# The first gate and value units of a feed-forward up projection, run unit after unit or feature tile by feature tile over four PSUM accumulators

## The chip, the cores and the metric

The kernel runs on one NeuronCore of a Trainium2 chip, in one launch. The metric is device time in microseconds (us). The engines are TensorE (PE in the rows; PEld is its weight load), VectorE (DVE), ScalarE (ACT), GpSimd (POOL) and SyncE (SP, which here only issues DMAs). A stage is read on the profiled execution, and times are compared as medians of several executions.

## The reference

Two layers of a decoder block on 256 tokens of width 1024, in float32. The change touches only the first half of each layer's feed-forward part:

```python
for l in range(DEPTH):                                   # DEPTH = 2
    ...                                                  # attention of two kinds
    x = x + mixed @ w_out[l]
    h = rmsnorm(x, norm_ffn_g[l])
    g_in, u = jnp.split(h @ w_up[l], 2, axis=-1)         # 1024 -> 2 x 2816
    x = x + (jax.nn.silu(causal_dwconv(g_in, conv_w[l], conv_b[l])) * u) @ w_down[l]
```

`causal_dwconv` is a convolution of three taps over the tokens. The row factor of the norm, `rsqrt(mean(x*x) + eps)`, is one number per token.

## The kernel before, in words

Activations are kept features by tokens: `x` is `[128, 8, 256]`, eight feature tiles of 128 features with 256 tokens each. Float32 products are made of three passes: weights and activations are each split into a high part `hi` (rounded to the short float that TensorE takes at full rate) and a rest `lo`, and `hi*hi + hi*lo + lo*hi` is summed in PSUM. So every weight that arrives by DMA in a `raw` buffer (five buffers, half a unit each) is first cast by ScalarE (`hi`, L242) and then subtracted by VectorE (`lo`, L243). A weight unit holds 256 output features; `next_unit(3)` asks for two units beyond the current one and issues their casts and subtractions at once.

The feed-forward part of a layer:

- `out_proj` adds the attention's output to `x`, feature tile by feature tile (L1065, two instructions for a tile). After each tile, `feed` makes the tile's `u`: `hi` on ScalarE (L314), `lo` on VectorE (L315), and its squares (L337), which GpSimd and, for the last tile, VectorE (L345, tile `fin`) sum for the norm.
- `ffn_up` goes through 11 column tiles `c`. Each has a gate unit (columns of `g_in`) and a value unit (columns of `u`), and each unit two halves of 128 columns. A half is 8 feature tiles k times 3 passes, 24 matmuls of 128x256 in one PSUM accumulator. `u` is not yet multiplied by the norm's row factor; that comes on the way out of PSUM.
- `rstd_col` forms the factor per token: two matmuls sum `fin` over the features (L356), VectorE (L358), GpSimd (a power, L359) and ScalarE (two diagonal blocks `dg`, L363). `rstd_row` spreads it over all partitions with one matmul (L369) and a ScalarE copy (`rb`, L371).
- `post_g` takes the gate unit out of PSUM (`g = acc * rb`, L1093), convolves it (L1096, L1097, L1099), forms the silu (L1101, L1102) and multiplies by `rb` again on GpSimd (L1103). The value unit is multiplied in (L1117) and the result is split into `act` (L300).

For c = 0 the kernel has an order of its own: the gate unit's two halves take turns feature tile by feature tile, one in an `acc` buffer, one in an `att` buffer, since the last tiles of `u` are still being made. Then comes the value unit, and in it, as hooks in front of matmul 3, 27 and 33, `rstd_col`, `rstd_row` and `post_g(0)`. For c > 0 a unit's two halves share one `acc` buffer, one half after the other.

PSUM has eight banks: the pool `acc` has three buffers, the pool `att` five. `out_proj` uses one `acc` buffer for each feature tile. The program is laid down in the order of the code, but a scheduler of the framework then orders each engine's instructions by its own estimates; each engine runs them strictly in that order. With c = 1 and on, the loop has settled into a pattern that repeats for each c.

Of the kernel before, what the change touches and what calls it, by code (L numbers as in the profile page):

```python
# [15 lines left out]
ALU = mybir.AluOpType  # L16
# [3 lines left out]
P = 128  # L20
D = 1024
S = 256
# [142 lines left out]
def block_kernel(ctx, tc, x_in, xo_in, ws, g_norm, g_rope, pos, w2, conv, rope_c, ropec_c, mask_c, misc_c, out):  # L165
    nc = tc.nc
    V, A, G, T = nc.vector, nc.scalar, nc.gpsimd, nc.tensor
# [5 lines left out]
    def acc():  # L173
        t = acc_p.tile([P, 512], F32, name="acc")
        return t

    def att():
        t = att_p.tile([P, 512], F32, name="att")
        return t
# [38 lines left out]
    def prepare(upto):  # L218
        while nxt[0] < len(units) and nxt[0] <= upto:
            i = nxt[0]  # L220
            u = units[i][1:]
            ffn = u[0] in ("up", "down")
            if ffn and ffn_pool[0] is None:
                return
            if u[0] == "w1":
                split[i] = [load_half(i, c0, UW // 2) for c0 in (0, UW // 2)]
                nxt[0] += 1
                continue
            w = _unit_width(u)
            pool, nb = (ffn_pool[0], 1) if ffn and ffn_turn(i) else (com, 2)  # L230
            hi = pool.tile([P, UW], F32R, name="hi", bufs=nb)
            lo = pool.tile([P, UW], F32R, name="lo", bufs=nb)
            step = w // 4 if (i, w // 4) in early else w // 2
            for c0 in range(0, w, step):
                if (i, c0) in early:
                    raw = early.pop((i, c0))
                else:
                    raw = load_half(i, c0, step)
                c = slice(c0, c0 + step)

                def halve(h=hi[:, c], l=lo[:, c], r=raw):
                    A.copy(h, r)  # L242
                    V.tensor_sub(l, r, h.bitcast(F32))  # L243
                pend.append((i, halve))
            split[i] = (hi, lo)
            nxt[0] += 1
# [3 lines left out]
    def flush(upto):  # L250
        while pend and pend[0][0] <= upto:
            pend.popleft()[1]()

    def next_unit(ahead=2):
        i = ui[0]
        ui[0] += 1
        flush(i)
        prepare(i + ahead - 1)
        flush(i)
        if ahead != 2 or units[i][1] in ("up", "down", "out") :  # L260
            flush(i + ahead - 1)
        return split.pop(i)
# [35 lines left out]
    def split_evac(hi, lo, src):  # L298
        A.copy(hi, src)
        V.tensor_sub(lo, src, hi.bitcast(F32))  # L300
# [3 lines left out]
    def new_u(pool=com, name="hT"):  # L304
        u = pool.tile([P, 2, 8, S], F32R, name=name)
        sums.clear()
        return u
# [59 lines left out]
    def rstd_row():  # L367
        ps = att()
        T.matmul(ps[:, 0:S], ones, sums["dg"], start=True, stop=True)  # L369
        rb = com.tile([P, S], F32, name="rb", bufs=1)  # L370
        A.copy(rb, ps[:, 0:S])  # L371
        return rb

    def run(mms, hooks={}):
        for i, f in enumerate(mms):
            if i in hooks:
                hooks[i]()
            f()

    def feat_major(o, hi, lo, src, ms, nk):  # L380
        todo = []
        for k in range(nk):
            todo += [(o, hi[:, k, ms], src[:, 0, k], k == 0, False), (o, hi[:, k, ms], src[:, 1, k], False, False),
                     (o, lo[:, k, ms], src[:, 0, k], False, k == nk - 1)]
        return [lambda a=a: T.matmul(a[0], a[1], a[2], start=a[3], stop=a[4]) for a in todo]  # L385
# [684 lines left out]
    def ffn_up(l, pool, u, act):  # L1070
        cw = pool.tile([P, NFT, 4], F32, name="cw")
        nc.sync.dma_start(cw, conv[l].rearrange("p (f i) -> p f i", i=4))
        box = {}

        def unit(hooks, first=False):
            hi, lo = [z.rearrange("p (k n) -> p k n", k=8) for z in next_unit(3)]
            p1 = acc()
            outs = [p1[:, 0:S], att()[:, 0:S] if first else p1[:, S:]]
            lists = [feat_major(outs[mt], hi, lo, u, slice(mt * P, (mt + 1) * P), 8) for mt in range(2)]
            if first:  # L1080
                mms = [f for i in range(0, 24, 3) for ls in lists for f in ls[i:i + 3]]
            else:
                mms = lists[0] + lists[1]
            run(mms, hooks)
            return outs if first else [p1]

        def post_g(c, p1):
            z = pool.tile([P, 2, S], F32, name="z", bufs=3)
            g = pool.tile([P, 2, S], F32, name="g", bufs=2)
            rb = box["rb"][:, None, :].to_broadcast([P, 2, S])  # L1090
            for i, z1 in enumerate(p1):
                n = 2 // len(p1)
                V.tensor_tensor(g[:, i * n:(i + 1) * n], z1.rearrange("p (a q) -> p a q", a=n), rb[:, :n], op=ALU.mult)  # L1093
            for mt in range(2):
                f = 2 * c + mt
                A.activation(z[:, mt], g[:, mt], AF.Identity, bias=cw[:, f, 3:4], scale=cw[:, f, 2:3])  # L1096
                V.scalar_tensor_tensor(z[:, mt, 1:], g[:, mt, :S - 1], cw[:, f, 1:2], z[:, mt, 1:],  # L1097
                                       op0=ALU.mult, op1=ALU.add)
                V.scalar_tensor_tensor(z[:, mt, 2:], g[:, mt, :S - 2], cw[:, f, 0:1], z[:, mt, 2:],  # L1099
                                       op0=ALU.mult, op1=ALU.add)  # L1100
            A.activation(g, z, AF.Tanh, scale=0.5)  # L1101
            V.scalar_tensor_tensor(z, g, 1.0, z, op0=ALU.add, op1=ALU.mult)  # L1102
            G.tensor_tensor(z, z, rb, op=ALU.mult)  # L1103
            box["z"] = z

        def second(c, pg):
            return {10: lambda: post_g(c, pg)}

        for c in range(11):
            if c == 0:  # L1110
                pg = unit({}, True)
                pu = unit({3: rstd_col, 27: lambda: box.update(rb=rstd_row()), 33: lambda: post_g(0, pg)})
            else:
                pg = unit({})
                pu = unit(second(c, pg))
            z = box["z"]
            V.tensor_tensor(z, z, pu[0].rearrange("p (a q) -> p a q", a=2), op=ALU.mult)  # L1117
            split_evac(act[:, 0, 2 * c:2 * c + 2], act[:, 1, 2 * c:2 * c + 2], z)

    def ffn_down(l, act):  # L1120
# [47 lines left out]
    for l in range(DEPTH):  # L1168
        with tc.tile_pool(name=f"attn{l}", bufs=1, reuse_waits="tile") as pool:
            mT = attention_layer(l, pool, hT)  # L1170
        with tc.tile_pool(name=f"ffn{l}", bufs=1, reuse_waits="tile") as pool:
            ffn_pool[0] = pool
            u = new_u(pool, "u")
            act = pool.tile([P, 2, NFT, S], F32R, name="act")
            pad = pool.tile([P, 16], F32, name="pad")
            G.memset(pad, 0.0)
            hT = out_proj(l, u, mT)
            ffn_up(l, pool, hT, act)
            hT = ffn_down(l, act)
            ffn_pool[0] = None  # L1180
# [32 lines left out]
```

## Time and profile before

| | us |
|---|---|
| median of 3 runs (954.5 to 956.36) | 955.96 |
| profiled execution, its own time | 956.27 |
| span in the profile, first to last instruction | 954.5 |
| PE busy (share of the span) | 934.4 (98%) |
| DVE busy | 762.1 (80%) |
| ACT busy | 570.0 (60%) |
| POOL busy | 151.8 (16%) |
| busy share of the DMA queue that brings the weights | 52.3% of 16 engines |

An engine's busy time is the time in which one of its instructions runs. Matmuls are pipelined and their ends are modelled, so the gaps between matmuls are better read from their starts than from the busy share. Starts in the rows are in us from the span's start; the first layer's feed-forward part begins at 297.49 and the second layer's at 768.95.

### The profile page before, as it was taken

The numbers are of one execution on the slowest core, as the hardware profiler recorded it, in microseconds if no ns is written. First come the engines' busy times: TensorE is split into PE (matmuls) and PEld (weight loads), VectorE is DVE, ScalarE is ACT, GpSimd is POOL, SyncE is SP. The second block draws the span as 40 slices with busy tenths as digits, with TensorE's granted clock in tenths as the row PEclk, the third lists the DMA queues.
The fourth block names the chain that finished last, engine by engine and source line by source line (L and its number), as shares of the span: only waits on it lengthen the run. The fifth ranks groups of instructions, "written<-read, shape, count | busy, mean of one in ns | idle before, by whom it ended". The sixth has DMA issues, their size and how long they took to land.

```text
span 954.5 us, 18604 instructions
## 1 busy us (share of the span) xinstructions
PE 934.4 (98%) x7102; PEld 851.2 (89%) x7102; DVE 762.1 (80%) x1722; ACT 570.0 (60%) x1164; POOL 151.8 (16%) x177
## 2 busy tenths in 40 slices
PE   8999999999999999999999999999999999999998
PEld 6778887879999999999988787878799999999998
DVE  5999967987778899986569998688976988988742
ACT  5768756665556555555456876576645655555431
POOL 2230112221002111110143311131300121111000
DMA  8643456435457565666455335644354565666660
GB/s 288 238 142 123 160 178 229 140 111 167 154 154 228 182 201 179 200 197 198 145 170 197 113 118 198 209 144 161 117 181 155 161 221 176 198 196 199 198 209 19
DMA packets 48330, 165.95 MB, mean 174 GB/s; under 512 B 6128, under 2 KB 7664, under 8 KB 48112
## 3 DMA queue, kind: packets, MB, share of 16 engines
q1 hardware_dynamic: 46656, 163.17, 52.3%
q10 hardware_dynamic: 1584, 1.59, 0.5%
q8 instruction: 56, 0.92, 0.4%
q14 instruction: 34, 0.28, 0.1%
HBM read 163.69 MB, written 1.05 MB: 173 GB/s over the span
## 4 chain that ended last, share of the span: by engine, by line
PE 75%; DVE 13%; ACT 6%; DMA 2%; issue 2%; POOL 2%; ACTq 0%; DVEq 0%; POOLq 0%
PE acc L385 26%; PE acc L296 5%; PE acc L294 5%; PE acc L295 5%; DVE lo L243 5%; PE acc L1131 4%; PE acc L1133 4%; PE acc L1132 4%; PE att L620 3%; PE att L625 3%; PE acc L1006 2%; PE acc L1008 2%; PE acc L1007 2%; ACT hi L242 2%; PE acc L1042 2%
## 5 line engine op out<-in xcount | busy, mean ns | idle before, releaser
L243 DVE TENSOR_TENSOR lo<-raw,hi 128x1024 fp32r<-128x1024 f32 (+2 forms) x294 | 369.0, 1271 | 54.5 <-ACT hi L242 52.5
L242 ACT CAST hi<-raw 128x1024 fp32r<-128x1024 f32 (+2 forms) x294 | 293.9, 1030 | 163.0 <-PE acc L295 52.8
L385 PE MATMUL acc<-u,hi 128*128 128x256 f32 x1376 | 238.4, 278 | 1.2 <-DVE u L315 1.2
L385 PEld LDWEIGHTS acc<-u,hi 128*128 128x128 f32 x1376 | 208.1, 188 | 1.8 <-DVE u L315 1.6
L385 PE MATMUL acc<-u,lo 128*128 128x256 f32 x688 | 190.5, 277 | 0.0
L294 PE MATMUL acc<-hi,hT 128*128 128x512 f32 (+1 forms) x384 | 152.6, 397 | 2.7 <-ACT hi L242 2.7
L296 PE MATMUL acc<-lo,hT 128*128 128x512 f32 (+1 forms) x384 | 149.0, 389 | 4.9 <-DVE lo L243 4.9
L295 PE MATMUL acc<-hi,hT 128*128 128x512 f32 (+1 forms) x384 | 147.4, 385 | 0.0
L385 PEld LDWEIGHTS acc<-u,lo 128*128 128x128 f32 x688 | 129.1, 188 | 0.0
L1133 PE MATMUL acc<-act,lo 128*128 128x256 f32 x352 | 97.2, 276 | 0.0
L1131 PE MATMUL acc<-act,hi 128*128 128x256 f32 x352 | 97.2, 276 | 0.0
L1132 PE MATMUL acc<-act,hi 128*128 128x256 f32 x352 | 97.2, 276 | 0.0
L296 PEld LDWEIGHTS acc<-lo,hT 128*128 128x128 f32 x384 | 72.2, 188 | 21.9 <-DVE lo L243 7.7
L294 PEld LDWEIGHTS acc<-hi,hT 128*128 128x128 f32 x384 | 72.3, 188 | 19.1 <-ACT hi L242 4.4
L295 PEld LDWEIGHTS acc<-hi,hT 128*128 128x128 f32 x384 | 72.4, 189 | 12.3
L1008 PE MATMUL acc<-hT,lo 128*128 128x256 f32 x256 | 71.8, 281 | 1.2 <-DVE lo L243 1.1
L1006 PE MATMUL acc<-hT,hi 128*128 128x256 f32 x256 | 72.8, 284 | 0.0
L1007 PE MATMUL acc<-hT,hi 128*128 128x256 f32 x256 | 71.6, 280 | 0.0
L1132 PEld LDWEIGHTS acc<-act,hi 128*128 128x128 f32 x352 | 66.1, 188 | 0.0
L1133 PEld LDWEIGHTS acc<-act,lo 128*128 128x128 f32 x352 | 66.1, 188 | 0.0
L1131 PEld LDWEIGHTS acc<-act,hi 128*128 128x128 f32 x352 | 66.1, 188 | 0.0
L1103 POOL TENSOR_TENSOR z<-z,rb 128x512 f32<-128x512 f32 x22 | 30.4, 1383 | 203.3 <-DVE z L1102 203.3
(214 smaller groups left out, 1694.7 us busy)
## 6 DMA issues: line engine op xcount, KB each, us to landing
raw<-in_ws_dram SPq DMA_DIRECT2D x298, 512.0 KB, 4.5
raw<-in_ws_dram SPq DMA_DIRECT2D x8, 280.0 KB, 4.7
raw<-in_ws_dram SPq DMA_DIRECT2D x4, 256.0 KB, 6.0
x<-in_x_dram SPq DMA_DIRECT2D x1, 1024.0 KB, 9.0
out_dram<-x ACTq DMA_DIRECT2D x8, 128.0 KB, 2.1
gr<-in_g_rope_dram SPq DMA_DIRECT2D x2, 384.0 KB, 5.8
masks<-in_mask_dram SPq DMA_DIRECT2D x1, 576.0 KB, 5.7
xo<-in_xo_dram ACTq DMA_DIRECT2D x2, 256.0 KB, 5.6
```

What stands on the lines that cost most here:

```text
L242: A.copy(h, r)
L243: V.tensor_sub(l, r, h.bitcast(F32))
L294: T.matmul(o, a_hi, b_hi, start=first, stop=False)
L295: T.matmul(o, a_lo, b_hi, start=False, stop=False)
L296: T.matmul(o, a_hi, b_lo, start=False, stop=last)
L385: return [lambda a=a: T.matmul(a[0], a[1], a[2], start=a[3], stop=a[4]) for a in todo]
L1006: T.matmul(o, hi[:, k, ms], hT[:, 0, k], start=k == 0, stop=False)
L1007: T.matmul(o, hi[:, k, ms], hT[:, 1, k], start=False, stop=False)
L1008: T.matmul(o, lo[:, k, ms], hT[:, 0, k], start=False, stop=k == 7)
L1131: T.matmul(ps, hi[:, c], act[:, 0, k], start=k == 0, stop=False)
L1132: T.matmul(ps, hi[:, c], act[:, 1, k], start=False, stop=False)
L1133: T.matmul(ps, lo[:, c], act[:, 0, k], start=False, stop=k == NFT - 1)
```

## The change

For c = 0 the gate unit and the value unit become one run of 96 matmuls over four accumulators: two `att` buffers for the gate halves (`pg`), two `acc` buffers for the value halves (`pu`). For each feature tile the three passes of all four halves follow each other. The hook for `rstd_col` stands in front of matmul 84 of the 96 (that is, ahead of the last feature tile), the one for `rstd_row` in front of matmul 90, and `post_g(0)` is issued after the run. The multiplication by the value unit takes one instruction for each accumulator, so two for c = 0. Lines behind the change are shifted: L1093 becomes L1100, L1096 to L1103 become L1103 to L1110, and L1117 becomes L1125.

```diff
-        def unit(hooks, first=False):
+        def lists(outs):
             hi, lo = [z.rearrange("p (k n) -> p k n", k=8) for z in next_unit(3)]
+            return [feat_major(outs[mt], hi, lo, u, slice(mt * P, (mt + 1) * P), 8) for mt in range(2)]
+
+        def unit(hooks):
             p1 = acc()
-            outs = [p1[:, 0:S], att()[:, 0:S] if first else p1[:, S:]]
-            lists = [feat_major(outs[mt], hi, lo, u, slice(mt * P, (mt + 1) * P), 8) for mt in range(2)]
-            if first:
-                mms = [f for i in range(0, 24, 3) for ls in lists for f in ls[i:i + 3]]
-            else:
-                mms = lists[0] + lists[1]
+            a, b = lists([p1[:, 0:S], p1[:, S:]])
+            run(a + b, hooks)
+            return [p1]
+
+        def first_two():
+            pg, pu = [[f()[:, 0:S] for _ in range(2)] for f in (att, acc)]
+            ls = lists(pg) + lists(pu)
+            mms = [f for i in range(0, 24, 3) for z in ls for f in z[i:i + 3]]
+            hooks = {84: rstd_col, 90: lambda: box.update(rb=rstd_row())}
             run(mms, hooks)
-            return outs if first else [p1]
+            post_g(0, pg)
+            return pu
...
             if c == 0:
-                pg = unit({}, True)
-                pu = unit({3: rstd_col, 27: lambda: box.update(rb=rstd_row()), 33: lambda: post_g(0, pg)})
+                pu = first_two()
             else:
                 pg = unit({})
                 pu = unit(second(c, pg))
             z = box["z"]
-            V.tensor_tensor(z, z, pu[0].rearrange("p (a q) -> p a q", a=2), op=ALU.mult)
+            for i, p1 in enumerate(pu):
+                n = 2 // len(pu)
+                V.tensor_tensor(z[:, i * n:(i + 1) * n], z[:, i * n:(i + 1) * n], p1.rearrange("p (a q) -> p a q", a=n),
+                                op=ALU.mult)
```

How the instructions stand after the scheduler, in the first layer (the second reads the same). A row names the line, the operation, output<-inputs and the output's shape; in brackets are the engines (or DMA queues) whose counters it waits on.

**Place 1, TensorE, the beginning of the feed-forward part.** `acc_3642` is the last feature tile of `out_proj`, `hi_3600`/`lo_3601` the gate unit of c = 0. Before, with the gate halves in `acc_3697` and `att_3698`:

```order
L385 MATMUL acc_3642<-hT_3240,lo_3527 128x256
L385 MATMUL acc_3697<-u_3371,hi_3600 128x256 [waits DVE_49,PE_49]
L385 MATMUL acc_3697<-u_3371,hi_3600 128x256
L385 MATMUL acc_3697<-u_3371,lo_3601 128x256
L385 MATMUL att_3698<-u_3371,hi_3600 128x256 x2
L385 MATMUL att_3698<-u_3371,lo_3601 128x256
```

Now, with the gate halves in `att_3677`, `att_3678` and the value halves in `acc_3679`, `acc_3680` (weights `hi_3681`/`lo_3682`):

```order
L385 MATMUL acc_3642<-hT_3240,lo_3527 128x256
L385 MATMUL att_3677<-u_3371,hi_3600 128x256 x2
L385 MATMUL att_3677<-u_3371,lo_3601 128x256
L385 MATMUL att_3678<-u_3371,hi_3600 128x256 x2
L385 MATMUL att_3678<-u_3371,lo_3601 128x256
L385 MATMUL acc_3679<-u_3371,hi_3681 128x256 [waits DVE_49,PE_49,Activation_49]
L385 MATMUL acc_3679<-u_3371,hi_3681 128x256
L385 MATMUL acc_3679<-u_3371,lo_3682 128x256 [waits DVE_49]
L385 MATMUL acc_3680<-u_3371,hi_3681 128x256 [waits DVE_49,PE_49]
L385 MATMUL acc_3680<-u_3371,hi_3681 128x256
```

The run begins in two `att` buffers without a wait, and within the first feature tile it opens two `acc` buffers. By the counts that they wait for, `acc_3679` follows the L1065 instructions that read feature tile 5 of `out_proj`, and `acc_3680`, at matmul 9 of the 96, those that read feature tile 6.

**Place 2, ScalarE and TensorE, the norm's row factor.** ScalarE before, from the last cast of the gate unit of c = 1 (`hi_3683`) over the casts of the value unit of c = 1 (`hi_3747`) to `rb`:

```order
L242 CAST hi_3683<-raw_3687 128x1024 [waits DMAHW4_49]
L242 CAST hi_3747<-raw_3749 128x1024 [waits DMAHW5_49,PE_49]
L242 CAST hi_3747<-raw_3751 128x1024 [waits DMAHW6_49]
L363 ACTIVATE dg_3768<-ident_70,rstd_3764 128x128 [waits Pool_49]
L363 ACTIVATE dg_3768<-ident_70,rstd_3764 128x128
L371 COPY rb_3797<-att_3795 128x256 [waits PE_49]
L1096 ACTIVATE z_3805<-g_3806,cw_3675 128x256 [waits DMAHW7_49,DVE_49]
```

ScalarE now, where `hi_3687` is the gate unit of c = 1, `hi_3701` the value unit of c = 1, and `hi_3839` the gate unit of c = 2:

```order
L242 CAST hi_3687<-raw_3691 128x1024 [waits DMAHW4_49]
L363 ACTIVATE dg_3802<-ident_70,rstd_3798 128x128 [waits Pool_49]
L242 CAST hi_3701<-raw_3703 128x1024 [waits DMAHW5_49,PE_49]
L242 CAST hi_3701<-raw_3705 128x1024 [waits DMAHW6_49]
L363 ACTIVATE dg_3802<-ident_70,rstd_3798 128x128
L242 CAST hi_3839<-raw_3841 128x1024 [waits DMAHW7_49,PE_49]
L371 COPY rb_3813<-att_3811 128x256 [waits PE_49]
L242 CAST hi_3839<-raw_3843 128x1024 [waits DMAHW0_49]
```

Two casts now stand between the two halves of `dg`, and a third ahead of `rb`. On TensorE the spreading matmul L369, which waits for the second half of `dg`, now stands in the gate unit of c = 1 (`acc_3838`), behind 14 of its 48 matmuls:

```order
L385 MATMUL acc_3838<-u_3371,lo_3688 128x256
L385 MATMUL acc_3838<-u_3371,hi_3687 128x256 [waits Activation_49]
L385 MATMUL acc_3838<-u_3371,hi_3687 128x256
L369 MATMUL att_3811<-dg_3802,ones_68 128x256 [waits Activation_49]
L385 MATMUL acc_3838<-u_3371,lo_3688 128x256 [waits DVE_49]
L385 MATMUL acc_3838<-u_3371,hi_3687 128x256 x2
```

Before, L369 stood in the value unit of c = 0, in front of its matmul 27.

**Place 3, VectorE, from the row factor to the gate units.** Before:

```order
L360 TENSOR_SCALAR rstd_3764<-rstd_3764 128x2 [waits Pool_49]
L243 TENSOR_TENSOR lo_3748<-raw_3749,hi_3747 128x1024 [waits DMAHW5_49,Activation_49]
L243 TENSOR_TENSOR lo_3748<-raw_3751,hi_3747 128x1024 [waits DMAHW6_49,Activation_49]
L1093 TENSOR_TENSOR g_3806<-acc_3697,rb_3797 128x256 [waits Activation_49]
L1093 TENSOR_TENSOR g_3806<-att_3698,rb_3797 128x256
```

Now:

```order
L360 TENSOR_SCALAR rstd_3798<-rstd_3798 128x2 [waits Pool_49]
L243 TENSOR_TENSOR lo_3702<-raw_3703,hi_3701 128x1024 [waits DMAHW5_49,PE_49,Activation_49]
L243 TENSOR_TENSOR lo_3702<-raw_3705,hi_3701 128x1024 [waits DMAHW6_49,Activation_49]
L243 TENSOR_TENSOR lo_3840<-raw_3841,hi_3839 128x1024 [waits DMAHW7_49,PE_49,Activation_49]
L1100 TENSOR_TENSOR g_3822<-att_3677,rb_3813 128x256 [waits Activation_49]
L1100 TENSOR_TENSOR g_3822<-att_3678,rb_3813 128x256
L243 TENSOR_TENSOR lo_3840<-raw_3843,hi_3839 128x1024 [waits DMAHW0_49,Activation_49]
L1104 SCALAR_TENSOR_TENSOR z_3821<-g_3822,cw_3675,z_3821 128x255 [waits Activation_49] x2
L1106 SCALAR_TENSOR_TENSOR z_3821<-g_3822,cw_3675,z_3821 128x254 [waits DVE_49] x2
L1100 TENSOR_TENSOR g_3919<-acc_3838,rb_3813 128x512 [waits PE_49]
```

Ahead of the first L1100 there is one subtraction more, and the gate unit of c = 1 (last row) comes out of PSUM behind all of that. The value unit of c = 1 now takes the `acc` buffer of the gate unit of c = 1: its first matmul waits for a count that VectorE reaches with that last row. Before, it took the `acc` buffer of the gate unit of c = 0 and waited for the first L1093.

## Rows read from the trace of the kernel before

**Rows 1.** Windows: us, busy us of PE, PEld, DVE, ACT, POOL (instructions), granted clock, DMA share, GB/s.

```profile
0.00:954.50 954.50, 934.40 (x7102) 851.16 (x7102) 762.15 (x1722) 570.03 (x1164) 151.81 (x177) 1.00 0.53 174
322.30:768.90 446.60, 440.78 (x3340) 400.16 (x3339) 362.79 (x832) 272.76 (x565) 77.09 (x84) 1.00 0.53 171
```

**Rows 2.** Timeline of PE, first layer: start, us, operation, count, idle before and releaser.

```profile
297.49 0.40 PE L385 MATMUL acc<-u,hi 128*128 128x256 f32 x2
...
302.44 0.38 PE L385 MATMUL acc<-u,hi 128*128 128x256 f32 x1
303.66 0.38 PE L385 MATMUL acc<-u,hi 128*128 128x256 f32 x1 [0.84 <-DVE u L315]
...
304.70 0.50 PE L356 MATMUL att<-ones,fin 128*128 128x1 f32 x4
...
305.50 0.40 PE L385 MATMUL acc<-u,hi 128*128 128x256 f32 x2
...
307.97 0.59 PE L369 MATMUL att<-dg,ones 128*128 128x256 f32 x2
...
308.75 0.40 PE L385 MATMUL acc<-u,hi 128*128 128x256 f32 x2
...
310.87 0.40 PE L385 MATMUL acc<-u,hi 128*128 128x256 f32 x2
...
315.11 0.40 PE L385 MATMUL acc<-u,hi 128*128 128x256 f32 x2
```

**Rows 3.** Timeline of PE, second layer.

```profile
768.95 0.40 PE L385 MATMUL acc<-u,hi 128*128 128x256 f32 x2
...
773.89 0.28 PE L385 MATMUL acc<-u,hi 128*128 128x256 f32 x1
774.53 0.39 PE L385 MATMUL acc<-u,hi 128*128 128x256 f32 x1 [0.36 <-DVE u L315]
```

**Rows 4.** Timeline of DVE, first layer.

```profile
299.51 0.66 DVE L1065 SCALAR_TENSOR_TENSOR x<-acc,x 128x128 f32<-128x128 f32 x2
...
305.24 0.16 DVE L358 TENSOR_SCALAR rstd<-att 128x2 f32<-128x2 f32 x1 [0.15 <-PE att L356]
...
309.01 0.42 DVE L1093 TENSOR_TENSOR g<-acc,rb 128x256 f32<-128x256 f32 x1 [0.35 <-ACT rb L371]
...
318.18 0.68 DVE L1093 TENSOR_TENSOR g<-acc,rb 128x512 f32<-128x512 f32 x1
318.78 2.35 DVE L243 TENSOR_TENSOR lo<-raw,hi 128x1024 fp32r<-128x1024 f32 x2
321.05 0.87 DVE L1097 SCALAR_TENSOR_TENSOR z<-g,cw,z 128x255 f32<-128x255 f32 x2
321.84 0.87 DVE L1099 SCALAR_TENSOR_TENSOR z<-g,cw,z 128x254 f32<-128x254 f32 x2
```

**Rows 5.** Timeline of DVE, second layer: the row that answers to 299.51.

```profile
770.37 0.67 DVE L1065 SCALAR_TENSOR_TENSOR x<-acc,x 128x128 f32<-128x128 f32 x2
```

**Rows 6.** Timeline of ACT, first layer.

```profile
304.44 2.00 ACT L242 CAST hi<-raw 128x1024 fp32r<-128x1024 f32 x2 [0.82 <-PE att L385]
306.34 0.69 ACT L363 ACTIVATE dg<-ident,rstd 128x128 f32<-128x128 f32 x2
308.60 0.37 ACT L371 COPY rb<-att 128x256 f32<-128x256 f32 x1 [1.56 <-PE att L369]
```

**Rows 7.** Timeline of POOL, first layer.

```profile
305.48 0.70 POOL L359 TENSOR_TENSOR rstd<-rstd,mhalf 128x2 f32<-128x2 f32 x1 [3.57 <-DVE rstd L358]
313.94 2.22 POOL L1103 TENSOR_TENSOR z<-z,rb 128x512 f32<-128x512 f32 x1 [7.77 <-DVE z L1102]
```

**Rows 8.** Line L211, the loads of `raw`, whole span.

```profile
DMA to landing us min/median/max: 3.0/4.5/9.7
```

**Rows 9.** Timeline of PE in `out_proj`, first layer: two rows with 37 groups of three matmuls between.

```profile
284.45 0.28 PE L385 MATMUL acc<-hT,lo 128*128 128x256 f32 x1
...
297.03 0.28 PE L385 MATMUL acc<-hT,lo 128*128 128x256 f32 x1
```

## The prediction

> **What bounds the kernel now.** I read the windows first: TensorE (PE) is busy 934.4 of 954.5 us at a granted clock of 1.00, the other engines 80% or less [rows 1]. So PE's own gaps are what a change can win or lose, and I went to its timeline where the feed-forward part begins. The reader is to see one gap in each layer. In the first, a matmul starts at 302.44 and the next at 303.66 [rows 2]. From 310.87 to 315.11 twelve groups of three matmuls start, 0.353 us a group, 0.118 a matmul, so 1.10 of that 1.22 is a wait, for the last feature tile of `u`. In the second layer it is 773.89 to 774.53, less 0.12: 0.52 [rows 3]. These 1.62 us are all that the change can win. From 304 to the end of `ffn_down` in the first layer PE has no gap; between 322.3 and 768.9 it idles 446.60 - 440.78 = 5.8 us in all [rows 1].
>
> **What goes.** With four accumulators 84 matmuls stand ahead of the last feature tile in place of 42. PE reaches it some 5 us later than now, behind the 1.10 and 0.52 by far. The full 1.62 us go.
>
> **What comes, first wait (A): a PSUM buffer at matmul 9.** `acc_3680` (place 1) needs VectorE's second L1065 of feature tile 6 in `out_proj`. That pair runs from 299.51 to 300.17 [rows 4]; nothing ahead of it on VectorE or ScalarE changes place. PE reaches matmul 9 at 297.49 + 9 x 0.118 = 298.55. For a hand-over between engines I take 0.08 us (L358 ends at 305.40, GpSimd's L359 starts at 305.48 [rows 4, 7]). So PE stands still until 300.25: 1.70 us. In the second layer the pair ends at 771.04 [rows 5], PE is there at 768.95 + 1.06 = 770.01 [rows 3]: 1.11 us. PE takes matmuls in the order given, so the three accumulators that are free wait too. Before, only one `acc` buffer was opened here, and the next one 48 matmuls later.
>
> **Second wait (B): the row factor.** L356 now stands behind 84 of the 96 matmuls: 300.25 + 25 groups x 0.353 = 309.08, against 304.70 [rows 2]. L356 costs PE 305.50 - 304.70 - 0.353 = 0.45, as before; with the four groups left the gate unit of c = 1 starts at 309.08 + 0.45 + 1.41 = 310.94, about where it does now (310.87), and L369 is still to come. The chain behind L356, with the durations of now: L358 starts 0.54 later (305.24 - 304.70), L359 0.24 after that and lasts 0.70, so `dg` can start at 310.64. One half of `dg` takes 0.35 (0.69 for two [rows 6]), to 310.99. Then ScalarE does the two casts of place 2, 0.95 each (304.44 to 306.34), to 312.89, and only then the second half, to 313.24; PE can have L369 at 313.32. Its place is reached at 310.94 + 14 x 0.118 = 312.59: a wait of 0.73. Before, the casts ran ahead of `dg` while L359 ran, and L369, 27 matmuls down, found `dg` ready. That cover is gone because L356 comes when ScalarE has long run out of casts.
>
> **Third wait (C): the buffer of the next gate unit.** The value unit of c = 1 needs L1100 of c = 1 (place 3). L369 costs PE 308.75 - 307.97 - 0.353 = 0.43 [rows 2], as before; 34 matmuls are left of the gate unit, which ends at 313.32 + 0.43 + 4.01 = 317.76. On VectorE an instruction starts about 0.08 before the listed end of the one ahead (318.86 and 318.78 [rows 4]), so a subtraction takes (321.05 - 318.78) / 2 = 1.135, a half of L1100 0.42 - 0.08 = 0.34, the four convolution steps 322.71 - 321.05 - 0.08 = 1.58, and a whole L1100 0.68. The third cast of place 2 runs from 313.24 to 314.29 (one takes 2.00 - 0.95 = 1.05). Then VectorE: subtraction from 314.37 to 315.51, the two L1100 halves to 316.19 (`rb`, 0.63 behind L369 by rows 2 and 6 but behind that cast, is there at 314.6), subtraction to 317.32, convolution to 318.90, L1100 of c = 1 to 319.58. PE goes on at 319.66: a wait of 1.90. Even with VectorE free it could not be under 0.08 + 0.68 + 0.08 = 0.84, since a unit now takes the buffer of the unit just ahead of it.
>
> B and C hang on L356 alone, so they are the same in the second layer.
>
> **What costs nothing.** The two L1125 of c = 0 take 0.08 to 0.16 more on VectorE than one. They release the buffers of the gate and value units of c = 2. By the same chain GpSimd's multiplication (L1110) starts at 321.40; behind a running subtraction it takes 2.22 [rows 7], so the first L1125 ends at 324.1. PE wants the buffer at 319.66 + 16 x 0.353 = 325.31. Cover: 1.1 us. From c = 2 on the waits read as before, and PE, with no gap, has nowhere to catch up.
>
> **The sum.** First layer 1.70 + 0.73 + 1.90 - 1.10 = +3.23; second 1.11 + 0.73 + 1.90 - 0.52 = +3.22; together +6.45. The profiled execution took 956.27 (span 954.5 and 1.8 around it), so 962.7 for one like it; it lies 0.3 above the median of 955.96, and by the median I predict **962.4**. Bounds of this case: 14 or so steps hang together in B and C of each layer; hand-overs of 0.02 instead of 0.08 in half of them take off 0.8 in both layers, subtractions at 1.23 instead of 1.135 and a later A add about as much; I take 960.8 to 964.0.
>
> **A rule on PSUM and the clock.** The first gate unit of now already changes its PSUM buffer after every three matmuls, at 0.353 a group (297.49 to 302.44, 14 groups), the same as the units that stay in one; the clock is 1.00 over the whole span [rows 1, 2]. By the rows four buffers cost nothing, and the sum is 962.4. The Trainium skill (TensorE: Matmul & The Clock Gate, section "A second HAM failure mode: psum-queue depth-cycling") tells of a kernel that went round its PSUM banks in every iteration, left TensorE briefly idle between groups of matmuls, and had the clock gate swing between its two levels; that speaks against the change, and no row here shows it. What it would make of the time is rival 3.
>
> **Rivals.**
> 1. *The chain is partly hidden*: B is nil and C at its least, 0.84. Against it: the casts stand between the halves of `dg` in the order. 955.96 + 2.81 + 1.68 - 1.62 = 958.8.
> 2. *A late load adds a fourth wait*: the second cast for the value unit of c = 2 needs a load that can start only when the subtraction of the value unit of c = 1 frees its buffer, at about 313.3. At the median of 4.5 [rows 8] it lands at 317.8, and the cast starts at 318.8. At the longest, 9.7, cast, tanh, L1109 (0.68 each, an estimate from the L1093 row), L1110 and L1125 end at about 328.4, 3.1 after PE wants the buffer; 968.6 if in both layers. It begins at a landing of about 6.6 us.
> 3. *The clock falls* to 1.2 GHz while PE goes through four buffers: 32 groups at twice 0.353, 11.3 us more in each layer, 985.0. Against it: a PE gap of 1.1 us left the clock at 1.00.
> 4. *Given back in the attention*: PE's 5.8 us of waits between the two feed-forward parts [rows 1] could take up the first layer's 3.23, if what PE waits for there were not late as well; it comes from chains that PE itself starts. 959.2.
> 5. *PE makes it up* (not slower): 480 groups (304 of `ffn_up`, 176 of `ffn_down`) follow C in a layer. In `out_proj` a group took (297.03 - 284.45) / 37 = 0.340 [rows 9]. If the weight loads, ahead after a stand-still, let PE run at that, it gains up to 6.4 us a layer; from 6.7 ns a group on (3.23 / 480) all is regained: 956.0, no change. Against it: after the wait of now, three groups take 304.70 - 303.66 = 1.04, as always.
>
> **Chances.** Forecast 0.78; rival 1 0.04; rival 2 0.06; rival 3 0.02; rival 4 0.04; rival 5 0.05; 0.01 for something faster that I do not see. This kernel's measurement can tell about 0.2% (1.9 us) from no change. The forecast and rivals 1 to 4 are slower by more (958.8 is 0.30%): 0.94; rival 5 within: 0.05. Range 958.9 to 966.0: it holds the forecast and rival 4 and leaves out 1, 2 in full, 3 and 5, 0.17.
>
> **What would show it.** Right: in PE's timeline no wait at the last feature tile; a matmul with about 1.4 (first layer) and 0.8 us of listed idle ahead of it near 300.2 and 771.1, released by L1065; L356 near 309; L369 waiting for `dg`; a wait of about 1.6 to 1.9 near 319.6, released by L1100; then no gap to the end of the layer. Wrong: L369 or the value unit of c = 1 starting without a wait; a gap near 325 (rival 2); a clock under 1.00 (rival 3); groups under 0.353 behind the waits (rival 5). My weakest term is C, since every step of VectorE's queue is in it.

## The result, and the profile after

The changed kernel takes 961.55 us (median of 6 runs, 959.69 to 961.86), the kernel before 955.86 (954.5 to 956.36) beside it: a ratio of 1.0058 (95% interval 1.0045 to 1.007), so slower, against 962.4 predicted. The profiled execution took 961.83 with a span of 960.0, 5.5 more than the span of before.

The table of TensorE's waits in the kernel after (waiting operation, whom it waits for, us in total, times, longest) has three rows that before had not, and no row for `u` any more:

```profile
PE acc L385 <- DVE x L1065: 3.2, 2, 1.6
PE acc L385 <- DVE g L1100: 3.1, 2, 1.6
...
PE att L369 <- ACT dg L363: 1.0, 2, 0.5
```

Two new waits for a PSUM buffer, one for the row factor, each once a layer. The same in time, in TensorE's timeline of the first layer, which answers to [rows 2]:

```profile
297.79 0.40 PE L385 MATMUL att<-u,hi 128*128 128x256 f32 x2
...
298.74 0.28 PE L385 MATMUL acc<-u,lo 128*128 128x256 f32 x1
300.61 0.48 PE L385 MATMUL acc<-u,hi 128*128 128x256 f32 x2 [1.59 <-DVE x L1065]
300.93 0.28 PE L385 MATMUL acc<-u,lo 128*128 128x256 f32 x1
...
309.26 0.39 PE L356 MATMUL att<-ones,fin 128*128 128x1 f32 x3
...
312.53 0.40 PE L385 MATMUL acc<-u,hi 128*128 128x256 f32 x2
313.41 0.48 PE L369 MATMUL att<-dg,ones 128*128 128x256 f32 x1 [0.49 <-ACT dg L363]
...
317.83 0.28 PE L385 MATMUL acc<-u,lo 128*128 128x256 f32 x1
319.67 0.50 PE L385 MATMUL acc<-u,hi 128*128 128x256 f32 x2 [1.56 <-DVE g L1100]
...
325.43 0.40 PE L385 MATMUL acc<-u,hi 128*128 128x256 f32 x2
```

The idle time in brackets begins at a modelled end; by starts, with 0.118 us a matmul, a wait is a little longer. The letters are those of the prediction. A, the `acc` buffer at matmul 9: 300.61 - 298.86 = 1.75. B, the row factor: 313.41 - 312.77 = 0.64. C, the buffer of the next gate unit: 319.67 - 317.95 = 1.72. The last row is the gate unit of c = 2, without a wait. The second layer answers to [rows 3]:

```profile
771.04 0.40 PE L385 MATMUL att<-u,hi 128*128 128x256 f32 x2
...
771.98 0.28 PE L385 MATMUL acc<-u,lo 128*128 128x256 f32 x1
773.84 0.47 PE L385 MATMUL acc<-u,hi 128*128 128x256 f32 x2 [1.58 <-DVE x L1065]
...
786.58 0.48 PE L369 MATMUL att<-dg,ones 128*128 128x256 f32 x1 [0.48 <-ACT dg L363]
...
792.84 0.39 PE L385 MATMUL acc<-u,hi 128*128 128x256 f32 x1 [1.56 <-DVE g L1100]
```

A is as long here as in the first layer (773.84 - 772.10 = 1.74). What TensorE waits for stands in the timeline of DVE, to hold against [rows 4]:

```profile
309.79 0.16 DVE L358 TENSOR_SCALAR rstd<-att 128x2 f32<-128x2 f32 x1 [4.41 <-PE att L356]
...
312.14 3.50 DVE L243 TENSOR_TENSOR lo<-raw,hi 128x1024 fp32r<-128x1024 f32 x3 [1.20 <-ACT hi L242]
315.55 0.75 DVE L1100 TENSOR_TENSOR g<-att,rb 128x256 f32<-128x256 f32 x2
316.21 1.22 DVE L243 TENSOR_TENSOR lo<-raw,hi 128x1024 fp32r<-128x1024 f32 x1
...
318.92 0.69 DVE L1100 TENSOR_TENSOR g<-acc,rb 128x512 f32<-128x512 f32 x1
...
323.67 0.75 DVE L1125 TENSOR_TENSOR z<-z,acc 128x256 f32<-128x256 f32 x2 [1.18 <-POOL z L1110]
```

and of ACT, to hold against [rows 6]:

```profile
310.77 0.40 ACT L363 ACTIVATE dg<-ident,rstd 128x128 f32<-128x128 f32 x1 [6.84 <-POOL rstd L359]
311.08 1.98 ACT L242 CAST hi<-raw 128x1024 fp32r<-128x1024 f32 x2
312.96 0.40 ACT L363 ACTIVATE dg<-ident,rstd 128x128 f32<-128x128 f32 x1
```

The two casts stand between the halves of `dg`, and L1100 of c = 1 ends at 319.61, where the chain of the prediction had 319.58. The clock, by the windows (columns as in [rows 1]):

```profile
297.50:325.00 27.50, 23.86 (x200) 23.23 (x199) 19.16 (x32) 13.31 (x22) 4.39 (x4) 1.00 0.57 195
325.00:420.00 95.00, 95.00 (x837) 95.00 (x836) 84.82 (x107) 53.78 (x71) 12.63 (x9) 1.00 0.59 187
```

TensorE idles 3.6 us in the stretch of the three waits, nothing for the 95 us behind it, at a clock of 1.00 in both. So by this trace the loss lies in those gaps; the experiments below take them away one by one.

### The profile page after: what moved, and what is told of

It reads as the page before. It is cut to its first block, busy times and chain, and to the rows that moved or that the text cites. A ratio compares the mean times of both kernels' runs of the same rounds, so it can differ in the third digit from the quotient of the medians.

```text
span 960.0 us, 18603 instructions
## 1 busy us (share of the span) xinstructions
PE 935.6 (97%) x7102; PEld 852.1 (89%) x7102; DVE 758.0 (79%) x1724; ACT 569.1 (59%) x1164; POOL 150.3 (16%) x177
## 4 chain that ended last, share of the span: by engine, by line
PE 73%; DVE 14%; ACT 6%; DMA 3%; POOL 2%; issue 2%; SPq 0%; ACTq 0%; DVEq 0%; POOLq 0%
PE acc L385 24%; DVE lo L243 5%; PE acc L296 5%; PE acc L294 5%; PE acc L295 5%; PE acc L1140 4%; PE acc L1141 4%; PE acc L1142 4%; PE att L620 3%; PE att L625 3%; PE acc L1006 2%; PE acc L1008 2%; ACT hi L242 2%; PE acc L1007 2%; DMA raw<-in_ws_dram 2%
## 5 line engine op out<-in xcount | busy, mean ns | idle before, releaser
L243 DVE TENSOR_TENSOR lo<-raw,hi 128x1024 fp32r<-128x1024 f32 (+2 forms) x294 | 367.4, 1266 | 56.6 <-ACT hi L242 55.5
L385 PE MATMUL acc<-u,hi 128*128 128x256 f32 x1344 | 231.7, 277 | 6.3 <-DVE x L1065 3.2
L385 PEld LDWEIGHTS acc<-u,hi 128*128 128x128 f32 x1344 | 202.8, 188 | 7.1 <-DVE g L1100 3.5
L385 PE MATMUL acc<-u,lo 128*128 128x256 f32 x672 | 186.6, 278 | 0.0
L385 PEld LDWEIGHTS acc<-u,lo 128*128 128x128 f32 x672 | 126.3, 188 | 0.1
L1110 POOL TENSOR_TENSOR z<-z,rb 128x512 f32<-128x512 f32 x22 | 32.3, 1466 | 198.8 <-DVE z L1109 198.8
```

## The experiments

Each kernel below computes the whole result. Its edit is against the changed kernel unless another is named; times are medians, each beside the kernel before on the same chip, and stages are read on the profiled execution of each. A ratio has its 95% interval in brackets. The expectations of e1 to e4 weigh three theories: W, that TensorE's waits for PSUM buffers and for `dg` are three things with a price each; R, that the late row factor is the root and the others follow from it; O, that the order of the matmuls itself costs.

**e1: A alone.** Tile 6 of `out_proj` in a buffer of the attention pool.

```diff
-                ps = acc()
+                ps = att() if mm == 6 else acc()
```

> Only the first wait (A) is taken away: feature tile 6 of out_proj uses an att buffer, so the second value half finds an acc buffer that was read long before. Three theories. Buffers (W): A, B and C add up, each as long as PE's own start times show (A 1.75 and 1.74 us in the two layers, B 0.64, C 1.72). Row factor (R): the loss is that L356 stands behind 84 matmuls, the buffer waits only show it. Order (O): going round four accumulators costs by itself, the waits are a by-product. W expects 961.55 - 3.49 = 958.1, the matmul near 300 with no wait, L356 about 1.7 earlier, B and C as long as they were. R expects about the same as W here, since L356 moves with PE. O expects 961.5.

957.99 beside 956.0, ratio 1.0021 [1.0012, 1.003]. TensorE's waits in this kernel:

```profile
PE acc L385 <- DVE g L1100: 3.1, 2, 1.6
...
PE att L369 <- ACT dg L363: 1.0, 2, 0.5
```

The row for L1065 is gone, the other two are as they were, and the time fell by 3.56, A's 1.75 + 1.74 = 3.49. As W, and as R, which expects about the same here; O falls.

**e2: C alone.** The value unit of c = 1 in a buffer of the attention pool.

```diff
-        def unit(hooks):
-            p1 = acc()
+        def unit(hooks, buf=acc):
+            p1 = buf()
...
-                pu = unit(second(c, pg))
+                pu = unit(second(c, pg), att if c == 1 else acc)
```

> Only the third wait (C) is taken away: the value unit of c = 1 uses an att buffer, so it need not wait until the gate unit of c = 1 is out of PSUM. Buffers (W): 961.55 - 2 x 1.72 = 958.1; A (about 1.75) and B (about 0.64) stay, no new wait, since the next units' buffers come free near 319.6 and 324.1 and PE wants them near 323.6 and 329. Row factor (R): c = 0 leaves PSUM as late as before, so the wait moves on to a later unit, 961.5. Order (O): 961.5.

960.38 beside 956.0, ratio 1.0047 [1.0034, 1.006]: 2.3 above W. The wait C is gone. But `ffn_down` of the first layer lasts from 421.96 to 482.73, 60.77 us where it took 59.84 before, and from the start of the second `ffn_down` to the end of the span it is 64.0 in place of 63.1. (`ffn_down` is the stage behind `ffn_up`; for each part of its output it reads all of `act`, so it also needs the tiles of the last c.) TensorE's timeline in the second `ffn_down` shows a wait that no kernel had so far:

```profile
902.58 0.28 PE L1140 MATMUL acc<-act,hi 128*128 128x256 f32 x1
903.34 0.38 PE L1141 MATMUL acc<-act,hi 128*128 128x256 f32 x1 [0.48 <-DVE act L300]
```

TensorE arrives before VectorE has written the last feature tiles of `act`. In the first layer the same place costs 0.12, and then 59 groups go at 0.353 us in place of 0.340 (0.8). In the profiled execution these are 0.93 and 0.9, together 1.8. They can't be set off against the 2.3 of the medians one for one: this execution, 961.61, is the slowest of the five, and in it TensorE also ran at a granted clock of 0.50 from 628 to 630, in the attention of the second layer.

**e3: A and C.** The second value half of c = 0 in the attention pool, which leaves an `acc` buffer free.

```diff
-            pg, pu = [[f()[:, 0:S] for _ in range(2)] for f in (att, acc)]
+            pg, pu = [[f()[:, 0:S] for f in fs] for fs in ((att, att), (acc, att))]
```

> The second value half of c = 0 uses an att buffer in place of an acc buffer, the order of the matmuls and the place of L356 stay. Buffers (W): A and C both go, because one acc buffer more is free afterwards; B (0.64) stays: 955.86 - 1.62 + 1.28 = 955.5, within the noise of the kernel before. Row factor (R): L356 still stands behind 84 matmuls, so most of C comes back at a later unit: 958 to 960. Order (O): still four accumulators in turn: 961.5.

955.98 beside 956.0, ratio 1.0004 [0.9995, 1.0013]. In the feed-forward part TensorE's waits are down to the one for `dg`:

```profile
PE att L369 <- ACT dg L363: 1.0, 2, 0.5
```

The interleaved order stands as in the changed kernel, and no loss is left that this measurement could tell: O and R fall. W had 955.5. In the profiled execution the two `ffn_down` take 60.1 (419.21 to 479.30) and 64.0 to the end of the span, 1.2 more than before in all, at the place that e2 showed: behind 20 groups TensorE stands for 0.1, and the 11 or 59 groups that follow go at 0.353.

**e8: A and C by the edits of e1 and e2 together.**

> Full result. The edits of e1 and e2 together (tile 6 of out_proj, and the value unit of c = 1, from the attention pool): A and C gone, B left, as in e3 but with other buffers. Waits (W): 961.55 - 1.75 - 1.74 - 2 x 1.72 = 954.6. The shortfall of e2 (it gained 1.2 where its two waits were 3.44) belongs to its edit: e1's and e2's gains add, 961.55 - 3.56 - 1.17 = 956.8. As e3, where 1.4 was given back: 956.0.

956.33 beside 955.95, ratio 0.9999 [0.9988, 1.001], with the same waits as e3. Two ways to free the buffers give the same time, 1.4 and 1.7 above what the measured waits add up to (954.6). By the median it can't be told whether e2's own shortfall is in it (956.8) or e3's (956.0). By the profile it is the same thing in all three: `ffn_down` takes 60.8 (420.07 to 480.83) and 63.4 to the end, again 1.2 more than before, with the same short stand behind 20 groups. What sets it is told at e11.

**e4: B alone, by an earlier row factor.**

```diff
-            hooks = {84: rstd_col, 90: lambda: box.update(rb=rstd_row())}
+            hooks = {48: rstd_col, 72: lambda: box.update(rb=rstd_row())}
```

> Only the place of the row factor is changed: rstd_col is hooked in front of matmul 48 of the 96 and rstd_row in front of matmul 72, so L356 stands near 305 as in the kernel before. The buffers stay those of the change; in the built order the value unit of c = 1 now takes the buffer of the first value half of c = 0 and waits for the first L1125. Buffers (W): B is gone, A stays (1.75), and the wait for L1125 is longer than C was, about 3.2 (the gate halves end near 310.8, then L1100, two subtractions, convolution, a subtraction, L1109, GpSimd's 2.2 and L1125, to 320.3, against 317.1 for PE): 961.55 + 2 x (3.2 - 1.72 - 0.64) = 963.2. Row factor (R): only A is left, 955.86 - 1.62 + 3.49 = 957.7. Order (O): 961.5.

966.21 beside 956.0, ratio 1.011 [1.0096, 1.0124], the opposite of R. L369 no longer waits. But the order on VectorE is another now, and the value unit of c = 1 stands in front of L1125, which waits for GpSimd. TensorE's timeline there:

```profile
316.42 0.28 PE L385 MATMUL acc<-u,lo 128*128 128x256 f32 x1
320.13 0.77 PE L385 MATMUL acc<-u,hi 128*128 128x256 f32 x2 [3.43 <-DVE z L1125]
320.69 0.41 PE L385 MATMUL acc<-u,lo 128*128 128x256 f32 x1
320.90 0.63 PE L385 MATMUL acc<-u,hi 128*128 128x256 f32 x2
```

W had that wait; the 3 us on top are for the most part in the groups behind it, 0.64 us each (320.69 to 321.33) where they had been 0.353, for some 4 groups here and 8 in the second layer. The windows say why:

```profile
320.00:330.00 10.00, 9.87 (x72) 9.90 (x73) 7.29 (x11) 4.23 (x6) 0.00 (x0) 0.85 0.48 161
...
795.00:805.00 10.00, 9.91 (x63) 9.95 (x64) 6.05 (x10) 3.26 (x6) 0.00 (x0) 0.70 0.53 165
```

TensorE is busy nearly all the time at a granted clock of 0.85 and 0.70: part of each stretch runs at the lower of the two levels, 1.2 GHz.

**e6: B alone, by its named cause.** `dg` on VectorE, so that no cast can stand between its halves.

```diff
-    def rstd_col():
+    def rstd_col(vec=False):
...
+            if vec:
+                V.tensor_scalar(dg[:, t * P:(t + 1) * P], ident, r[:, 1, t:t + 1], None, op0=ALU.mult)
+            else:
+                A.activation(dg[:, t * P:(t + 1) * P], ident, AF.Copy, scale=r[:, 1, t:t + 1])
...
-            hooks = {84: rstd_col, 90: lambda: box.update(rb=rstd_row())}
+            hooks = {84: lambda: rstd_col(True), 90: lambda: box.update(rb=rstd_row())}
```

> Full result. The changed kernel, with the two halves of dg on VectorE instead of ScalarE, so that no cast can stand between them; nothing else is moved. The named cause of B is tested alone. Casts (W): dg is ready some 0.6 us behind L360, L369 starts without a wait (B 0.64 gone), and as the subtraction for the value unit of c = 1 is no longer late, the gate unit's L1100 ends about 1 us sooner against TensorE, so C falls from 1.72 to about 0.7: 2 x (0.64 + 1.05) less than 961.55, 958.2. If only B goes and C grows by what B gave (C is VectorE's queue alone): 961.5. If C keeps its length: 960.3.

970.47 beside 955.95, ratio 1.0149 [1.0134, 1.0163]: all its numbers missed. (Lines from L364 on are 3 higher than in the changed kernel: L1128 is its L1125.) TensorE's waits, its timeline, and the window around the wait:

```profile
PE acc L388 <- DVE z L1128: 7.9, 2, 3.9
```

```profile
310.96 0.28 PE L388 MATMUL acc<-u,lo 128*128 128x256 f32 x1
311.70 0.70 PE L372 MATMUL att<-dg,ones 128*128 128x256 f32 x2 [0.45 <-DVE dg L364]
...
318.12 0.28 PE L388 MATMUL acc<-u,lo 128*128 128x256 f32 x1
322.35 0.77 PE L388 MATMUL acc<-u,hi 128*128 128x256 f32 x2 [3.95 <-DVE z L1128]
```

```profile
320.00:330.00 10.00, 7.65 (x46) 7.68 (x47) 6.25 (x11) 2.66 (x5) 2.76 (x2) 0.66 0.46 158
```

The value unit of c = 1 again took a buffer that L1125 frees, as in e4, and the clock was 0.66 from 320 to 330. `dg` was sooner: L369 (here L372) ran 2.12 us behind L356 (309.58 to 311.70), in the changed kernel 4.15 (309.26 to 313.41). But L369 itself had moved up 17 matmuls in the new order, from 26 to 9 behind L356, so it still waited.

**e9: e6 with the edit of e2**, to see whether that buffer was the whole of it.

> Full result. e6 (dg on VectorE) with the value unit of c = 1 in a buffer of the attention pool, the edit of e2. e6 took 970.47, and its trace shows a wait of 4.1 us in each layer in which that unit stands in front of the buffer of the first value half of c = 0 and waits for its L1125, with the granted clock down to 0.66 and 0.84 in the 10 us behind it, some 2.6 and 1.5 us of slower groups. Buffer (W): that choice of buffer is what e6 lost by; without it, and with A left and no C: 970.47 - 2 x 4.1 - 4.1 = 958.2, and the clock stays at 1.00 over the stretch. If dg on VectorE costs something by itself (VectorE later in every c), or the clock falls without the long wait: 962 or more. If the shortfall of e2 comes back: about 960.2.

957.05 beside 955.33, ratio 1.0018 [1.0009, 1.0026]; no wait for L1128, the clock at 1.00 over the stretch. It was the buffer. Where the 1.1 below expectation comes from is not shown: wait A is listed at 1.0 in both layers here and at 1.6 in e6, but `out_proj` ahead of it went at a slower pace, which takes 0.85 a layer back (both below).

**e5: none of the three, with an earlier row factor.** e3, and L356 and L369 in front of matmuls 60 and 84.

```diff
-            hooks = {84: rstd_col, 90: lambda: box.update(rb=rstd_row())}
+            hooks = {60: rstd_col, 84: lambda: box.update(rb=rstd_row())}
```

> Full result. The buffers of e3 (second value half from the attention pool: no wait A, no wait C) together with the row factor 24 matmuls earlier (L356 in front of matmul 60, L369 in front of matmul 84: no wait B, and matmul 60 lies behind the end of the sum of squares, 303.4 us in e3's trace). So TensorE has none of the three waits and has lost the wait of the kernel before too. Waits (W, the time moves by TensorE's waits in this stretch and by nothing else): e3's 955.98 less B in both layers, 2 x 0.64, is 954.7. Late chain (L, what TensorE gains here VectorE cannot follow, so it comes back as waits at the end of the stage or at the longer of the two paces): 955.6 or more, the same as e3, with a longer wait at the first group of ffn_down.

955.6 beside 955.95, ratio 0.9997 [0.9988, 1.0005]. From 297.73 to 418.67 TensorE works without a wait, 120.94 us for the first `ffn_up` and 120.92 for the second, against 123.04 and 122.45 before: 3.63 gained. `ffn_down` then takes 61.23 (418.67 to 479.90) in place of 59.84, and from the second `ffn_down` to the end of the span 65.2 in place of 63.1: 3.5 given back. In the first one, TensorE and then VectorE:

```profile
425.77 0.38 PE L1140 MATMUL acc<-act,hi 128*128 128x256 f32 x1
426.86 0.38 PE L1141 MATMUL acc<-act,hi 128*128 128x256 f32 x1 [0.70 <-DVE act L300]
```

```profile
424.39 0.68 DVE L1125 TENSOR_TENSOR z<-z,acc 128x512 f32<-128x512 f32 x1
424.99 1.22 DVE L243 TENSOR_TENSOR lo<-raw,hi 128x1024 fp32r<-128x1024 f32 x1
426.12 0.68 DVE L300 TENSOR_TENSOR act<-z,act 128x512 fp32r<-128x512 f32 x1
```

L300 of c = 10 ends at 426.80 and TensorE goes on at 426.86. As L: VectorE's chain of the last c did not come as much earlier as TensorE did.

**e7 and e10: e3 with `dg` on VectorE** (the same program, measured twice).

> Full result. e3 (no A, no C) with dg on VectorE as in e6, L356 and L369 where the change put them: the second way to have none of the three waits. Waits (W): e3's 955.98 less 2 x 0.64 = 954.7. Late chain (L): 955.6 or more. With e5 it shows whether a version without waits is faster than the kernel before, whichever way the wait for the row factor is taken away.

> Full result. The same program as e7 (dg on VectorE, second value half in the attention pool), measured again, since its gain is about as large as this kernel's measurement can tell. If e7's 0.9983 was no accident: a ratio of 0.997 to 0.9995, 953.5 to 955.5. If it was: 956.0, as e3.

954.47 beside 955.95, ratio 0.9983 [0.9973, 0.9993], and 954.44 beside 955.33, ratio 0.9989 [0.998, 0.9998]: faster than before, by as little as can be told. L369 still waits for `dg` (0.9 in all); `ffn_down` takes what it took before (59.85, 420.14 to 479.99 in e10).

**e11: e7 with L356 in front of matmul 75.**

```diff
-            hooks = {84: lambda: rstd_col(True), 90: lambda: box.update(rb=rstd_row())}
+            hooks = {75: lambda: rstd_col(True), 90: lambda: box.update(rb=rstd_row())}
```

> Full result. e7 with the row factor's column (L356) nine matmuls earlier, in front of matmul 75 instead of 84; L369 stays in front of matmul 90, and the orders of ScalarE and VectorE are the same as in e7. In e7 L369 still waits, by the starts about 0.65 us in each layer, for dg, which now comes 1.05 us sooner against TensorE. Waits (W): e7's 954.47 less 1.3 = 953.2. Late chain (L, VectorE cannot follow, as in e5, where 3.6 us gained in the two stages came back in ffn_down): 954.5 or more, with a wait for L300 at the first group of ffn_down.

953.63 beside 955.33, ratio 0.9981 [0.9972, 0.9991]; as W, and it beats the kernel before by 1.7 us. (L369 moved up too, to the front of matmul 90; in e7 it stood in front of matmul 93.) Its windows over the stretch of the waits and over the whole second `ffn_up`, and VectorE's last row for `act`:

```profile
297.50:325.00 27.50, 27.50 (x237) 27.45 (x237) 21.45 (x36) 14.60 (x22) 4.44 (x4) 1.00 0.62 206
766.95:888.49 121.54, 121.54 (x1065) 121.49 (x1063) 105.49 (x144) 67.84 (x92) 17.51 (x13) 1.00 0.61 195
```

```profile
425.30 0.68 DVE L300 TENSOR_TENSOR act<-z,act 128x512 fp32r<-128x512 f32 x1
```

TensorE has no gap. Both `ffn_up` stages take 121.54, 1.50 and 0.91 less than before, and the first `ffn_down` 59.85 (419.92 to 479.77). L300 of c = 10 starts at 425.30, 5.4 us behind the start of `ffn_down`; in e5 it started 7.45 behind.

The traces show how VectorE keeps up here and not in e5. Take its lag, from the end of a value unit on TensorE to the end of that unit's L300. In the first layer it is 6.15 us at c = 2 in the kernel before, 7.48 in e11, 8.29 in e3 and e8, and 9.52 in e5. From there it shrinks by about 0.18 with each c, but not below 5.91. At c = 10 it is 5.91 before, 6.05 in e11, 6.85 in e3 and 8.14 in e5. TensorE asks for the last tiles of `act` 6.8 us into `ffn_down`, behind 20 groups at 0.340: so before and e11 have no wait there, e3 and e8 have one of 0.1, and e5 has the long one. Why the lag at c = 2 differs was not tried.

## Why the prediction was right, and where a term was off

**What goes.** Right: no wait for `u`.

**A.** Right in the first layer (1.70, measured 1.75). In the second it was mis-sized: 1.11 predicted, 1.74 measured, the one term that was off by more than 0.2. I took TensorE's arrival and VectorE's end from the trace of before, where `out_proj` of that layer ran at 0.353 us a group of three matmuls; in the profiled run of after it ran at 0.340, as in the first layer [rows 9], so TensorE came sooner against VectorE. The runs bear it out: A is listed at 1.0 where `out_proj` ran at 0.353 (both layers of e4 and e9, the second of e2) and at 1.6 where it ran at 0.340 (both layers of after and e6, the first of e2). e1 shows that A costs its own length. The 0.63 by which A was longer in the second layer cost the total nothing, since `out_proj` ahead of it had been 0.85 shorter (below).

**B.** Right in its mechanism, 0.73 against 0.64: the casts stand between the halves of `dg` in ScalarE's rows. That they are the cause of the wait was tried in e6, which moved L369 as well and so did not settle it alone. Its trace still bears on it: with `dg` on VectorE L369 can run 2.12 behind L356 (e7 and e9 have 2.12 too), and the changed kernel reaches its place for L369 3.51 behind L356 (309.26 to 312.77). So without the casts L369 would have found `dg` ready there, an estimate from these two traces. e11, with `dg` on VectorE and L356 sooner, has no wait.

**C.** 1.90 against 1.72. Both sides of the wait hang on L356. Counted from it, TensorE's path to the value unit was right to 0.01 (8.68 predicted, 8.69 measured), and the chain over ScalarE and VectorE to the end of L1100 was 0.15 shorter than predicted (10.50, 10.35). That this end came within 0.03 of the forecast in absolute time is luck: L356 itself came 0.18 later than forecast (309.26 for 309.08). e3, e8 and e9 show that it is the buffer that costs, not the place in the order.

**What costs nothing.** Right: the first L1125 ends near 324.1, and the gate unit of c = 2 starts at 325.43 without a wait, a cover of 1.4 (the forecast's own times give 1.2, not 1.1). Rival 2 did not occur.

**The sum.** `ffn_up` grew by 2.94 in the first layer (297.79 to 423.77 against 297.49 to 420.53) and by 3.45 in the second, 6.39 where I had 6.45. That it came so close is in part luck: A's 0.68 too little stands against 0.54 too much in B and C, which makes 6.59. Behind A, 20 and 24 groups went at 0.340 (in the first layer between 300.93 and 309.26), 0.3 us a layer, so rival 5 is there at a tenth of what it needs, and only up to L356. It never had the room that the prediction gave it: in the first layer of before, 255 groups of `ffn_up` (from about 333.6 to 420.53) and the 176 of `ffn_down` (59.84 us) already went at 0.340, which leaves 49 of the 480, 0.7 a layer. The row that spoke against it was misread too: from 303.66 to 304.70 go eight matmuls, not three groups. The other way, each restart costs a little (300.61 to 300.93 is 0.32 where 0.24 is usual), 0.3 in all. Between the start of the first `ffn_down` and the second `ffn_up` 1.15 came back (347.27 in place of 348.42), which looks like rival 4 but for the most part isn't: 64 groups of `out_proj` at 0.340 in place of 0.353 are 0.85. The other 0.3 is open. 2.94 + 3.45 - 1.15 and 0.30 of a later start make 5.54, the 5.5 of the spans. The 1.15 and the 0.30, which the forecast had at nothing, are why its 6.45 lies 0.9 above what the span grew by.

**Rival 3.** It did not occur in the changed kernel: 32 groups went in turn through four buffers at a clock of 1.00, with no idle time between them but A. The kernel that the Trainium skill tells of (TensorE: Matmul & The Clock Gate, section "A second HAM failure mode: psum-queue depth-cycling") was briefly idle between groups time and again; this stretch shows neither that nor a swing of the clock. The price of the lower clock was real all the same, in e4 and e6, behind a long wait for a buffer.

## What to carry to other kernels

Before more PSUM accumulators are opened at once, ask of each buffer who read it last and when that reader comes in its own queue: TensorE goes in order, so one late buffer stops the three that are free. A small chain (here a row factor) that is moved behind more matmuls loses whatever hid it, and a chain that is made earlier can change which buffer a later unit gets; look at that first, since a wait of 1.7 us became one of 3.6 and one of 4.1. Where all waits are gone, look for the next engine's last result: in e5 TensorE's gain of 3.6 us came back there but for 0.1, and in e11 VectorE's last chain was in time.

## What was not expected of the hardware

**Two paces at full clock.** Groups of three 128x256 matmuls with their weight loads go at 0.340 or at 0.353 us, both at a granted clock of 1.00, and stay at one for tens to hundreds of groups. It is not the program alone: after and e4 have the same instructions up to the feed-forward part, and the first layer's `out_proj` goes at 0.340 in after and at 0.353 in e4:

```profile
284.08 0.28 PE L385 MATMUL acc<-hT,lo 128*128 128x256 f32 x1
...
297.00 0.28 PE L385 MATMUL acc<-hT,lo 128*128 128x256 f32 x1
```

```profile
284.35 0.28 PE L385 MATMUL acc<-hT,lo 128*128 128x256 f32 x1
...
296.72 0.28 PE L385 MATMUL acc<-hT,lo 128*128 128x256 f32 x1
```

That is 38 groups in 12.92 us, and 35 in 12.37. Waits often go with a switch (to 0.340 behind A, to 0.353 behind the small wait in e2's `ffn_down`), but before and after also switch to 0.340 at the beginning of the gate unit of c = 3 with no wait, and so does every other run that comes there at 0.353. What sets it stays open; 65 groups are worth 0.9 us, half of what a measurement of this kernel can tell.

**The clock behind a stand-still.** In the feed-forward part of after, waits of up to 1.75 us left the clock at 1.00. Behind those of 3.4 us in e4 and 3.9 in e6 (as listed) it fell, in all four cases, and 4 to 8 groups behind them went at about 0.64 us each. The length of one wait does not settle it, though. Near the start of after TensorE waited 2.52 for L243, until 25.61, and the granted clock is 0.50 from 26 to 29:

```profile
26.00:29.00 3.00, 3.00 (x15) 3.00 (x14) 2.27 (x11) 1.89 (x7) 1.06 (x2) 0.50 0.86 341
```

In e2 the 0.50 from 628 to 630 stands behind a wait of 1.42 (to 626.22, in the attention), while e5, with a wait of 2.48 that ends at 8.46, has 1.00 over its first 20 us. What decides is open.
